# Modulation from float32 blocks, and weight sums made by GpSimd during the input projection

## The chip, the cores and the metric

The kernel runs on one core of a Trainium2 chip. The metric is device time in microseconds (us) of one launch; the median of three runs before the change is 3407.99 us (3407.11 to 3412.31).

## The reference

Two layers of a transformer over 256 context and 1024 latent tokens of width 1024, all in float32. Per layer:

```python
mod = silu(c) @ ada_w + ada_b                     # six rows of 1024: shifts, scales, gates; once for c, once for c_ctx
z = (x * (1 + sc1) + sh1) @ w_in                  # 1024 -> 1984, split into q, kv, k_r, dq, dk, dv and a chunk part
y = concat(mla(q, kv), differential(dq, dk, dv), chunk_mix(zch)) @ w_o
x = layer_norm(ALPHA * x + g1 * y)
u = dwconv3((x * (1 + sc2) + sh2) @ ffn_wup)      # 1024 -> 5632 = gate and value
x = layer_norm(ALPHA * x + g2 * ((silu(gate) * val) @ ffn_wdown))    # 2816 -> 1024
```

## The kernel before, in words

**Arithmetic.** Large products are made from float32 operands that are split in two: `hi`, the value rounded to the fast type float32r (made by ScalarE, in `split`), and `lo`, the rest (`low`, on VectorE or GpSimd). `mm3` issues three matmuls for each product. A few small products are plain float32 matmuls: the chunk mixing in `post_z` (moving operand of 64 elements), the selector in `fin_diff`, `sumj` in `prep_Q`, and the selector `sel4` of the modulation. Every matmul has the line of `mm`, L447; the splits have the lines of `low` (L457) and `copy` (L460).

**Stages**, by the trace in us: start, with eight modulation pieces and the first product of the input projection (0 to 85); input projection of layer 0 (`in_proj`, to 285); attention (to 850); output projection (to 940); up projection (to 1600); down projection (to 1900); the same stages of layer 1 end at about 2080 (input), 2560 (attention), 2680 (output), 3160 (up) and 3410 (down).

**Modulation.** `mod_piece` makes 256 of the 6144 columns of `mod` for both conditioning vectors; there are 24 pieces a layer. A piece loads four blocks of 128x512 of `ada_w` (two of 128x1024 in the eight first ones), splits them, and runs 16 matmuls with the conditioning vector as stationary operand (`s4`: 128 rows x 4 columns) and 256 columns of weights as moving operand, four (or eight) to a task. The result, 4 rows of 256, is copied by ScalarE and brought into columns by two float32 matmuls with `sel4`; VectorE adds the bias (`fin`). Eight pieces stand in the start, 24 are spread over the attention of layer 0 and 16 over that of layer 1, as fillers with a low priority (`MODKEY`).

**Sums of weights.** The up and down projections use a fast matrix multiplication with seven products in place of eight, which needs sums of blocks of weights. Those of the down weights (`db`, four sums of 1408 x 512 a layer) are made by transfers: `sums` and `begin_sums` issue 16 DMAs a layer on GpSimd's queue during the attention, a copy (L591) and then one that adds to it (L592), in chunks of 704 rows. Those of the up weights (S1 to S4 of each of the 22 blocks) are added by VectorE in `up_operand` (`comb`, L1480) just ahead of their splits.

**Order.** `Sched.run` plays the program with a cost for each task, and issues each engine's instructions in the order that comes out; on the chip each engine then works strictly in that order. A task goes to the first of its allowed engines that is free (`either`: VectorE or GpSimd). Buffers come from shared pools: `M` (12 of 128x512), `L` (16 of 128x1024) and `S` among them.

Of the kernel before, what the change touches and what calls it, by code (L numbers as in the profile page):

```python
# [69 lines left out]
SUMROWS = 704  # L70
# [271 lines left out]
def pool_t(n):  # L342
    return {"pool": 2.1e-3 * n + 0.15}
# [47 lines left out]
class Kern:  # L391
# [185 lines left out]
    def flat(self, x, c):  # L577

        return x.rearrange("n p c -> (n p) c")[c * SUMROWS:(c + 1) * SUMROWS]

    def sums(self, l):

        x = self.db[l]
        w = lambda a, b: (lambda: self.i["w_down"][l, a, b])
        out = []

        def make(n, c, a, b, r=()):
            key = ("db", l, n, c)
            put = lambda: self.flat(x[n], c)
            kw = dict(w=[key], key=MODKEY, late=40.0)  # L590
            out.append(lambda: self.s.add({"pool": 1.0}, lambda e: self.nc.gpsimd.dma_start(out=put(), in_=self.flat(a(), c), max_dma_last_dim=2048), (), **kw))  # L591
            out.append(lambda: self.s.add({"pool": 1.0}, lambda e: self.nc.gpsimd.dma_start(out=put(), in_=self.flat(b(), c), accum_op=ALU.add, max_dma_last_dim=2048), [*r, key], **kw))  # L592

        for c in range(NP * P // SUMROWS):
            at = lambda n: ("db", l, n, c)
            make(0, c, w(0, 0), w(0, 1))
            make(1, c, w(0, 1), w(1, 1))
            make(2, c, w(1, 1), lambda: x[0], [at(0)])
            make(3, c, w(1, 0), lambda: x[2], [at(2)])
        return out  # L600

    def begin_sums(self, n):

        for f in self.due[:n]:
            f()
        del self.due[:n]

    def sum_chunks(self, name, l, n, f):
        a, b = f * P * 512, (f + 1) * P * 512 - 1
        m = SUMROWS * 512  # L610
        return [(name, l, n, c) for c in range(a // m, b // m + 1)]
# [28 lines left out]
    def setup(self):  # L640
# [9 lines left out]
        self.s4 = c.tile([P, KD, 4], F32R, tag="s4", name="s4")  # L650
        self.task(act_t(16), lambda e: nc.scalar.activation(s, cc, AF.Silu), ["cT"], ["silu"])
        self.task(dve_t(16), lambda e: nc.vector.tensor_copy(self.s4[:, :, 0:2], s), ["silu"], ["s4a"])
        self.task(dve_t(16), lambda e: self.low(nc.vector, self.s4[:, :, 2:4], s, self.s4[:, :, 0:2]), ["silu", "s4a"], ["s4"])
        self.sel4 = load("sel4", [4, 2])
# [21 lines left out]
        self.dc = d.tile([7, P, NP, P], F32, tag="dc", name="dc")  # L676
        self.db = [d.tile([4, NP, P, HALF], F32, tag=f"db{l}", name="db") for l in range(DEPTH)]
# [5 lines left out]
    def mod_piece(self, l, n, key=0, raws=None):  # L683
        nc = self.nc
        self.s.what = f"mod{l}"
        j, q = QUADS[n // 4], n % 4
        if raws:
            w = [self.weight(None, 1024, self.L, k=4, raw=raws[h]) for h in range(2)]
        else:
            src = [self.mod_src(l, n, h)[:, a:a + 512] for h in range(2) for a in (0, 512)]  # L690
            w = [self.weight(x, 512, self.M, k=2, key=key, acq=True) for x in src]
        kk = KD // len(w)
        ps, m4, pm = self.bank(), self.H(), self.bank(F32, (P, 2, 2))
        for h in range(len(w)):
            def go(e, h=h):
                for k in range(kk):
                    hi, lo = w[h][0][k]()
                    a = self.s4[:, kk * h + k]
                    self.mm(ps[:4, :256], a, hi, h + k == 0, False)
                    self.mm(ps[:4, :256], a, lo, False, kk * h + k == KD - 1)  # L700

            self.task(mm_t(2 * kk, 256), go, ["s4"] + w[h][1], [ps], key=key, acq=[m4] if h == 0 else ())
# [1311 lines left out]
```

## Time and profile before

| | |
|---|---|
| runs, us | 3407.11, 3412.31, 3407.99; median 3407.99 |
| profiled execution, us | 3411.25 |
| its span, first to last instruction, us | 3409.5 |
| mean granted TensorE clock | 0.967 of 2.4 GHz |
| busy: PE, DVE, ACT, POOL | 93%, 79%, 49%, 30% |
| DMA moved | 395 MB, of which 46 MB on GpSimd's queue |

PE is TensorE, PEld its weight loads, DVE VectorE, ACT ScalarE, POOL GpSimd, SP the engine that issues the other DMAs. PEclk is the granted share of TensorE's clock: 1.00 is 2.4 GHz, 0.50 is 1.2 GHz. Busy times of PE run to the modelled end of a matmul and overlap the next one, so the rate of a stretch is read from starts and counts.

### The profile page before, as it was taken

How to read it: one execution, taken by the hardware profiler on the slowest of the kernel's cores; microseconds unless marked ns; L12 is line 12 of the kernel's file. 1: busy time of each engine (PE TensorE's matmuls, PEld its weight loads, DVE VectorE, ACT ScalarE, POOL GpSimd, SP SyncE). 2: the span in 40 equal slices, each digit the busy share in tenths (PEclk: the TensorE clock that was granted, in tenths of full speed). 3: DMA queues.
4: the chain of work that ended last, by engine and by line, in shares of the span. 5: the costliest groups of instructions: out<-in, count | busy, mean ns of one | idle time of the engine just before them, and what ended most of it. 6: DMA issues, size and time to landing. Idle time of an engine off the chain costs nothing. (4 is left out here: it accounts for less than half of the span.)

```text
span 3409.5 us, 53373 instructions
## 1 busy us (share of the span) xinstructions
PE 3186.5 (93%) x18953; PEld 2785.7 (82%) x18953; DVE 2700.5 (79%) x6407; ACT 1677.3 (49%) x2944; POOL 1028.0 (30%) x631
## 2 busy tenths in 40 slices
PE   7999898998988999999999999989999889999997
PEld 5998887887987888887877898878889867877775
DVE  7567887999768787886687757988998788888687
ACT  5125665666244444544444325665662455545542
POOL 3002554543112111121133302554532232322143
PEclk9999998999999999999999999999999999999998
DMA  6214443442312223225663314353423122323672
GB/s 242 72 52 112 118 124 99 126 108 86 121 69 70 89 72 101 87 86 180 210 204 130 116 58 123 92 135 87 119 88 127 62 80 96 107 98 105 229 258 99
DMA packets 258548, 395.40 MB, mean 116 GB/s; under 512 B 63976, under 2 KB 115688, under 8 KB 258280
## 3 DMA queue, kind: packets, MB, share of 16 engines
q1 hardware_dynamic: 240872, 345.84, 31.4%
q0 software_dynamic: 17408, 46.14, 5.9%
q8 instruction: 149, 2.44, 0.3%
q14 instruction: 119, 0.97, 0.1%
HBM read 311.61 MB, written 126.42 MB: 128 GB/s over the span
## 5 line engine op out<-in xcount | busy, mean ns | idle before, releaser
L447 PE MATMUL t<-region 128*128 128x512 f32 (+4 forms) x15631 | 2853.0, 341 | 137.8 <-DVE region L457 55.0
L447 PEld LDWEIGHTS t<-region 128*128 128x128 f32 x15631 | 2442.1, 192 | 480.0 <-DVE region L457 69.2
L457 DVE TENSOR_TENSOR region<-region 128x512 fp32r<-128x512 f32 (+6 forms) x873 | 760.0, 893 | 176.2 <-ACT region L460 122.7
L460 ACT ACTIVATE region<-region 128x512 fp32r<-128x512 f32 (+4 forms) x944 | 593.9, 663 | 382.8 <-PE t L447 132.5
L460 ACT ACTIVATE region<-t 128x512 fp32r<-128x512 f32 (+4 forms) x948 | 462.1, 514 | 600.0 <-PE t L447 386.3
L457 POOL TENSOR_TENSOR region<-region 128x512 fp32r<-128x512 f32 (+7 forms) x283 | 392.3, 1398 | 1109.3 <-ACT region L460 714.8
L1480 POOL TENSOR_TENSOR region<-region 128x512 f32<-128x512 f32 (+3 forms) x132 | 248.6, 1889 | 823.6 <-DVE region L1667 518.5
L1188 ACT ACTIVATE region<-region,q 128x1280 f32<-128x1280 f32 (+1 forms) x216 | 273.5, 1267 | 175.7 <-DVE q L1187 169.7
L1183 DVE TENSOR_SCALAR_CACHE_REDUCE region<-t 128x512 f32<-128x512 f32 (+1 forms) x600 | 333.7, 584 | 21.3 <-PE t L447 19.1
L457 DVE TENSOR_TENSOR region<-t,region 128x512 fp32r<-128x512 f32 (+1 forms) x529 | 296.9, 595 | 52.8 <-ACT region L460 50.9
L1667 DVE SCALAR_TENSOR_TENSOR region<-region,conv 128x1023 f32<-128x1023 f32 x176 | 231.6, 1325 | 36.7 <-ACT region L1665 36.5
L1480 DVE TENSOR_TENSOR region<-region 128x512 f32<-128x512 f32 (+3 forms) x301 | 226.3, 770 | 2.5 <-DMA da<-region 1.4
L1252 PE MATMUL t<-ident,region 128*128 128x128 f32 x1312 | 184.8, 285 | 24.2 <-DVE region L1225 8.1
L1228 POOL TENSOR_TENSOR region<-region 128x1280 f32<-128x1280 f32 (+1 forms) x68 | 186.8, 2746 | 5.7
L1665 ACT ACTIVATE region<-region,conv 128x1024 f32<-128x1024 f32 x88 | 109.2, 1241 | 159.5 <-DVE region L1648 148.3
L1252 PEld LDWEIGHTS t<-ident,region 128*128 128x128 f32 x1312 | 154.9, 147 | 31.8 <-DVE region L1183 11.0
L1227 POOL TENSOR_SCALAR region<-region,q 128x1280 f32<-128x1280 f32 (+1 forms) x68 | 84.5, 1242 | 210.6 <-DVE q L1222 137.7
L447 PE MATMUL t<-region,s 128*4 128x256 f32 x768 | 119.1, 291 | 17.0 <-DVE region L457 9.2
L447 PEld LDWEIGHTS t<-region,s 128*4 128x4 f32 x768 | 64.6, 87 | 47.4 <-DVE region L457 12.5
L548 POOL TENSOR_TENSOR region<-region 128x1024 f32<-128x1024 f32 x26 | 73.7, 2847 | 95.9 <-DMA region<-n 67.7
L1008 DVE TENSOR_TENSOR region<-t,region 128x256 f32<-128x256 f32 x32 | 13.6, 424 | 107.4 <-PE t L447 107.4
L548 DVE TENSOR_TENSOR region<-region 128x1024 f32<-128x1024 f32 x34 | 62.3, 1841 | 18.2 <-DMA region<-n 17.7
(134 smaller groups left out, 1803.5 us busy)
## 6 DMA issues: line engine op xcount, KB each, us to landing
region<-in_wup SPq DMA_DIRECT2D x176, 256.0 KB, 3.0
region<-in_ada_w SPq DMA_DIRECT2D x160, 256.0 KB, 3.1
da<-region SPq DMA_DIRECT2D x154, 256.0 KB, 3.0
region<-da SPq DMA_DIRECT2D x154, 256.0 KB, 4.1
db<-in_w_down POOLq DMA_DIRECT2D x24, 1408.0 KB, 7.5
region<-db SPq DMA_DIRECT2D x88, 256.0 KB, 4.1
region<-in_w_down SPq DMA_DIRECT2D x66, 256.0 KB, 3.9
n<-region SPq DMA_DIRECT2D x26, 512.0 KB, 3.0
```

The source lines that it names most:

```text
L447: self.nc.tensor.matmul(ps, a, b, start=start, stop=stop, skip_group_check=again)
L457: eng.tensor_tensor(out=out, in0=full, in1=hi.bitcast(F32), op=ALU.subtract)
L460: self.nc.scalar.activation(out, in_, AF.Copy, **kw)
L548: self.task(engs or pool_t(D), lambda e, row=row, op=op: self.vec[e].tensor_tensor(out=x[:, :D], in0=x[:, :D], in1=row.t, op=op), [x, row] ...
L1183: self.task(dve_t(b - a), lambda e: nc.vector.tensor_scalar(p[:, a:b], ps[:, :b - a], -scale, None, op0=ALU.mult, op1=ALU.min, accum_out=n ...
L1188: self.task(act_t(nk, 0.19), lambda e: nc.scalar.activation(p[:, :nk], p[:, :nk], AF.Exp, bias=m.t, scale=-1.0, accum_out=s.t), [p, m], [p ...
L1227: nc.gpsimd.tensor_scalar(p2[:, :nk], p2[:, :nk], cc.t, 0.0, op0=ALU.mult, op1=ALU.add)
L1228: nc.gpsimd.tensor_tensor(out=p1[:, :nk], in0=p1[:, :nk], in1=p2[:, :nk], op=ALU.add)
L1252: nc.tensor.transpose(ps[:, u, j * P:(j + 1) * P], B[key][j][:, (kt + u) * P:(kt + u + 1) * P], self.ident)
L1480: self.task(engs or either(n), lambda e: self.vec[e].tensor_tensor(out=o(), in0=a(), in1=b(), op=op), r, w, **kw)
L1665: self.task(act_t(n, 0.15), lambda e: nc.scalar.activation(t.t, u(0, n), AF.Identity, scale=c[:, 1:2], bias=c[:, 3:4]), r + ["conv"], [t])
L1667: self.task(dve_t(n - 1, extra=0.06), lambda e, d=d: nc.vector.scalar_tensor_tensor(t[:, 1 - d:n - d], u(d, n - 1 + d), c[:, 2 * d:2 * d + ...
```

## The change

It has three parts.

1. **Modulation.** The blocks of `ada_w` are used as they are, as stationary float32 operands of 128x128, and the conditioning vectors (`silu`, 2 columns) move. A piece is one task of 16 float32 matmuls with a moving operand of 2 columns. The splits, `s4`, the copy and the selector matmuls are gone.
2. **Sums of down weights.** The 16 adding and copying DMAs a layer are gone. For each of the 11 blocks of down weights, four loads, four adds on GpSimd and four stores are issued among the tiles of the input projection.
3. **Sums of up weights.** For six of the 22 blocks a layer, S1 to S4 are made in the same way and stored in `ws`; the up projection loads them, and VectorE adds only for the other 16 blocks.

```diff
+UP_MADE = 6
...
-    def begin_sums(self, n):
...
+    def sums(self, name, l, m):
+        up = name == "ws"
+        out = (self.ws if up else self.db)[l]
+        src = self.i["wup" if up else "w_down"]
+        z = [self.L(F32, (P, 2, HALF)) for _ in range(2)]
+        for j in range(2):
+            for h in range(2):
+                self.dma(lambda j=j, h=h: z[j][:, h], lambda j=j, h=h: src[l, j, h, m], 4 * P * HALF, w=[(z[j], h)], key=MODKEY)
...
+        order = [("21", "22"), ("t0", "11"), ("21", "11"), ("t1", "12")] if up else [("11", "12"), ("12", "22"), ("t0", "22"), ("t2", "21")]
+        for n, (a, b) in enumerate(order):
+            self.task(pool_t(HALF), lambda e, n=n, a=a, b=b: self.vec[e].tensor_tensor(out=t[n].t, in0=q[a][0](), in1=q[b][0](), op=ALU.add), [q[a][1], q[b][1]], [t[n]], key=MODKEY)
+            self.dma(lambda n=n: out[n, m], lambda n=n: t[n].t, 4 * P * HALF, [t[n]], [(name, l, n, m)], key=MODKEY)
...
     def mod_piece(self, l, n, key=0, raws=None):
...
-                    self.mm(ps[:4, :256], a, hi, h + k == 0, False)
-                    self.mm(ps[:4, :256], a, lo, False, kk * h + k == KD - 1)
...
-                self.mm(pm[:, k], m4[:4, k * P:(k + 1) * P], self.sel4)
...
+        if not raws:
+            raws = [self.load(self.mod_src(l, n, h)[:, a:a + 512], 512, self.M, key) for h in range(2) for a in (0, 512)]
+        kk = KD // len(raws)
+        pm = self.bank(F32, (P, 2, 2))
+        def go(e):
+            for c in range(2):
+                for k in range(KD):
+                    o = k % kk * 256 + c * P
+                    self.mm(pm[:, c], raws[k // kk][:, o:o + P], self.silu[:, k], k == 0, k == KD - 1)
+        self.task({"pe": 1.8}, go, ["silu", *raws], [pm], key=key)
...
     def in_chunk(self, l, name, tabs):
...
+        for n, t in enumerate(tiles):
+            if name != "z" and n % 4 == 1 and self.pairs_due:
+                self.sums("db", l, self.pairs_due.pop(0))
+            if name != "z" and n % 4 == 3 and self.blocks_due:
+                self.sums("ws", l, self.blocks_due.pop(0))
...
     def up_load(self, l, m):
...
+            if f < UP_MADE:
+                todo = [n]
...
+                if x[0] == "S":
+                    j = int(x[1]) - 1
+                    src, r = self.ws[l][j, f], [("ws", l, j, f)]
...
     def up_operand(self, l, m):
...
-        if n[0] == "S":
+        if n[0] == "S" and f >= UP_MADE:
```

**The order on TensorE, where the attention of layer 0 begins** (`s_70` is `s4`, `sel_71` is `sel4`; the last number of a row counts matmuls of the program). Before:

```order
L447 MATMUL t<-region,s_70 4x256 x16
L447 MATMUL t<-sel_71,region 128x2 x2
L447 MATMUL t<-region 128x512 x12
L447 MATMUL t<-region 128x256 x24
L447 MATMUL t<-region,sumj 128x256
L447 MATMUL t<-region 128x256 x27
L447 MATMUL t<-region,s_70 4x256 x12
```

And with the change:

```order
L447 MATMUL t<-silu,region 128x2 x48
L959 MATMUL t<-ident,region 128x128 x6
L447 MATMUL t<-region 128x512 x12
L447 MATMUL t<-region 128x256 x24
L447 MATMUL t<-region,sumj 128x256
L447 MATMUL t<-region 128x256 x27
```

Three whole pieces now stand in a row here; of the 37 others in the attention, two stand together and 35 stand alone, each 16 matmuls without a break, where a piece was in parts of four to sixteen.

**The order on TensorE at the very start**, with the change:

```order
L447 MATMUL t<-silu,region 128x2 x64
L447 MATMUL t<-region 128x512 x36
L447 MATMUL t<-silu,region 128x2 x48
L447 MATMUL t<-region 128x512 x36
L447 MATMUL t<-silu,region 128x2 x16
L447 MATMUL t<-region 128x512 x96
```

The eight pieces stand where they stood before, as runs of 4, 3 and 1 pieces between the first products of the input projection.

**The order on GpSimd in the input projection of layer 0.** Before, with the first DMA at its end and others further on:

```order
L457 TENSOR_TENSOR region<-region 128x768
L929 TENSOR_TENSOR region<-region 128x256 x2
L938 TENSOR_TENSOR region<-region 128x256
L457 TENSOR_TENSOR region<-region 128x1280
L1017 TENSOR_TENSOR region<-region 128x256
L457 TENSOR_TENSOR region<-region 128x1152
L591 DMA db<-in_w_down 704x512
```

And with the change (L591 is now the add of `sums`, L903 the gain in `post_z`):

```order
L591 TENSOR_TENSOR region<-region 128x512 x2
L903 TENSOR_TENSOR region<-region 128x256
L591 TENSOR_TENSOR region<-region 128x512
L903 TENSOR_TENSOR region<-region 128x256
L591 TENSOR_TENSOR region<-region 128x512 x2
L903 TENSOR_TENSOR region<-region 128x256 x2
L591 TENSOR_TENSOR region<-region 128x512 x16
L457 TENSOR_TENSOR region<-region 128x768
L591 TENSOR_TENSOR region<-region 128x512 x44
L457 TENSOR_TENSOR region<-region 128x1152
L591 TENSOR_TENSOR region<-region 128x512 x3
```

All 68 adds of a layer stand ahead of GpSimd's first work for the attention, four gains of `post_z` stand among them, and no DMA is left on this queue.

## Rows read from the trace of the kernel before

**Rows 1.** The page: its first line.
```profile
span 3409.5 us, 53373 instructions
```

**Rows 2.** Busy time by stage: start:end, length, busy us and count by engine, PEclk, DMA.
```profile
core 0: us, PE busy (x) PEld busy (x) DVE busy (x) ACT busy (x) POOL busy (x), PEclk, DMA share, GB/s
0.00:85.00 85.00, 64.79 (x328) 48.07 (x328) 65.08 (x118) 50.27 (x67) 27.36 (x18) 0.94 0.69 243
...
114.00:285.00 171.00, 171.00 (x1286) 170.65 (x1286) 90.89 (x450) 41.24 (x114) 12.41 (x12) 1.00 0.26 76
285.00:850.00 565.00, 513.04 (x3582) 456.39 (x3580) 484.47 (x1455) 354.07 (x699) 261.58 (x173) 0.95 0.40 109
850.00:1100.00 250.00, 226.42 (x1583) 210.39 (x1584) 185.72 (x501) 104.08 (x168) 48.01 (x38) 0.95 0.25 83
...
1900.00:2080.00 180.00, 175.21 (x1265) 171.32 (x1264) 106.93 (x482) 43.64 (x110) 22.47 (x18) 0.98 0.29 87
2080.00:2560.00 480.00, 445.54 (x3121) 396.21 (x3119) 434.14 (x1233) 301.08 (x561) 221.51 (x137) 0.97 0.40 107
```

**Rows 3.** Groups on PE, shapes apart: two of 285:850, then two of 2080:2560.
```profile
L447 PE MATMUL t<-region,s 128*4 128x256 f32 x381 | 60.3, 291 | 5.2 <-DVE region L457 4.0 <-ACT region L460 1.1
L447 PE MATMUL t<-sel,region 4*128 4x2 f32 x96 | 15.0, 257 | 1.2 <-ACT region L460 0.6 <-DVE region L457 0.5
...
L447 PE MATMUL t<-region,s 128*4 128x256 f32 x244 | 38.0, 286 | 3.6 <-DVE region L457 3.6
L447 PE MATMUL t<-sel,region 4*128 4x2 f32 x64 | 9.6, 251 | 2.3 <-ACT region L460 2.3
```

**Rows 4.** Timeline of PE in the start: start, us, what, count, [idle before].
```profile
6.55 0.37 PE L447 MATMUL t<-region,s 128*4 128x256 f32 x1 [6.55 <-ACT region L460]
...
21.15 0.60 PE L447 MATMUL t<-sel,region 4*128 4x2 f32 x4 [0.52 <-ACT region L460]
...
38.96 2.20 PE L447 MATMUL t<-region,s 128*4 128x256 f32 x16
41.09 0.60 PE L447 MATMUL t<-sel,region 4*128 4x2 f32 x4
...
85.23 35.03 PE L447 MATMUL t<-region 128*128 128x64 f32 x190 [7.48 <-issue]
```

**Rows 5.** Busy time by stretch, as rows 2, for five short stretches.
```profile
35.60:41.60 6.00, 5.97 (x49) 4.15 (x47) 3.31 (x5) 4.80 (x7) 3.81 (x2) 1.00 0.81 286
85.20:88.60 3.40, 3.37 (x16) 3.40 (x16) 3.40 (x21) 0.00 (x0) 0.00 (x0) 0.50 0.00 0
95.10:98.20 3.10, 3.10 (x15) 2.57 (x14) 3.02 (x14) 0.00 (x0) 0.72 (x1) 0.99 0.35 140
419.40:429.60 10.20, 6.19 (x33) 6.19 (x34) 1.32 (x2) 1.38 (x3) 3.74 (x3) 0.50 0.59 200
467.20:470.60 3.40, 3.40 (x16) 3.10 (x15) 3.40 (x17) 3.18 (x7) 0.45 (x1) 0.50 0.57 155
```

**Rows 6.** Timeline of POOL, 400:435, as rows 4.
```profile
421.11 0.70 POOL L591 DMA_DIRECT2D db<-in_w_down  x1 [10.19 <-issue]
421.82 3.04 POOL L457 TENSOR_TENSOR region<-region 128x640 fp32r<-128x640 f32 x2
```

**Rows 7.** PE's waits in 285:850, then in 2080:2560: total us, times, longest.
```profile
PE t L1117 <- POOL region L457: 14.0, 2, 7.5
...
PE t L447 <- POOL region L457: 5.0, 1, 5.0
```

**Rows 8.** Groups of 285:850, shapes apart: two on DVE, one on POOL, one on ACT.
```profile
L457 DVE TENSOR_TENSOR region<-t,region 128x512 fp32r<-128x512 f32 x174 | 112.1, 680 | 25.0 <-ACT region L460 24.6
...
L457 DVE TENSOR_TENSOR region<-region 128x512 fp32r<-128x512 f32 x32 | 28.6, 901 | 0.4 <-ACT region L460 0.3
...
L457 POOL TENSOR_TENSOR region<-region 128x512 fp32r<-128x512 f32 x62 | 82.7, 1345 | 142.1 <-ACT region L460 127.5 <-PE t L1252 7.4 <-DVE q L1220 5.2
...
L460 ACT ACTIVATE region<-region 128x512 fp32r<-128x512 f32 x95 | 57.2, 628 | 0.2
```

**Rows 9.** The page, groups of the whole run: VectorE's and GpSimd's adds.
```profile
L1480 POOL TENSOR_TENSOR region<-region 128x512 f32<-128x512 f32 (+3 forms) x132 | 248.6, 1889 | 823.6 <-DVE region L1667 518.5
...
L1480 DVE TENSOR_TENSOR region<-region 128x512 f32<-128x512 f32 (+3 forms) x301 | 226.3, 770 | 2.5 <-DMA da<-region 1.4
```

More of the change, by code (lines that the diff above doesn't have):

```diff
@@ L574, in row_from_col @@
         return row
[L577 to L600, printed above, removed]
@@ L676, in setup @@
         self.dc = d.tile([7, P, NP, P], F32, tag="dc", name="dc")
+        self.ws = [d.tile([4, UP_MADE, P, HALF], F32, tag=f"ws{l}", name="ws") for l in range(DEPTH)]
         self.db = [d.tile([4, NP, P, HALF], F32, tag=f"db{l}", name="db") for l in range(DEPTH)]
@@ L686, in mod_piece @@
         j, q = QUADS[n // 4], n % 4
[L687 to L698, printed above, removed]
-                    self.mm(ps[:4, :256], a, hi, h + k == 0, False)
-                    self.mm(ps[:4, :256], a, lo, False, kk * h + k == KD - 1)
-            self.task(mm_t(2 * kk, 256), go, ["s4"] + w[h][1], [ps], key=key, acq=[m4] if h == 0 else ())
-        self.task(act_t(256), lambda e: self.copy(m4[:4], ps[:4, :256]), [ps], [m4], key=key)
-        def sel(e):
-            for k in range(2):
-                self.mm(pm[:, k], m4[:4, k * P:(k + 1) * P], self.sel4)
-        self.task({"pe": 0.25}, sel, [m4, "sel4"], [pm], key=key)
+        if not raws:
[8 more added lines that the diff above has]
+        self.task({"pe": 1.8}, go, ["silu", *raws], [pm], key=key)
         ks = slice(2 * q, 2 * q + 2)
@@ L843, in in_proj @@
         tabs = self.tabs if l == 0 else self.z_tables(l)
+        self.pairs_due, self.blocks_due = list(range(NP)), list(range(UP_MADE))
         for name in ZCH:
@@ L891, in in_chunk @@
             tiles = (8, 9, 0, 1) if l == 0 else (6, 7, 8, 9, 2, 3, 4, 5)
-        for t in tiles:
+        for n, t in enumerate(tiles):
[3 more added lines that the diff above has]
+                self.sums("ws", l, self.blocks_due.pop(0))
             r = self.in_tile(l, name, t, wk, wb, tabs)
@@ L1902, in program @@
             ada = [lambda a=a: self.mod_piece(*a, MODKEY) for a in ada]
-            self.due = self.sums(l)
-            m, d = len(ada), len(self.due)
-            fill = []
-            for j, a in enumerate(ada):
-                fill += [lambda: self.begin_sums(1)] * ((j + 1) * d // m - j * d // m) + [a]
-            self.attention(l, fill)
+            self.attention(l, ada)
             self.out_tiles(l, NT, True)
@@ L1997, in _arrays @@
     a["sel64"] = np.tile(np.eye(64, dtype=np.float32), (2, 1))
-    a["sel4"] = np.tile(np.eye(2, dtype=np.float32), (2, 1))
     return {k: np.ascontiguousarray(v) for k, v in a.items()}
```

36 lines of the change are left out of this document (16 added, 20 removed).

## The prediction, made before the changed kernel had run

> **What bounds the kernel now.** The page gives a span of 3409.5 us [rows 1]; the profiled execution itself took 3411.25 us, 3.3 above the median of the runs, 3407.99. The sum below is made against 3411.25 and 3 is taken off at its end.
>
> I read the busy time by stage next, since the mean over the span hides which engine sets which stage [rows 2]. The reader is to see that TensorE sets the input projection almost alone: 171.0 us busy of 171 in layer 0, 175.2 of 180 in layer 1, with VectorE near half. In the attention TensorE is busy 513.0 of 565 us and 445.5 of 480, with a clock of 0.95 and 0.97, and VectorE 484.5 and 434.1: two engines close to full, so what TensorE gains or loses there counts nearly in full and what VectorE gains counts in part. The first 250 us of the up projection have TensorE at 226.4 and VectorE at 185.7. Then come the groups of the modulation, TensorE's start, short stretches around falls of its clock, and the waits on GpSimd, each where it is needed.
>
> **The new piece of modulation.** Forty pieces stand in the attention, where TensorE is near the bound, 24 in layer 0 and 16 in layer 1. An old piece took 2.13 us of wide matmuls and 0.60 for its selector in an undisturbed place at full clock, 2.7 together [rows 4]. By busy time it is (60.3 + 15.0) / 24 = 3.1 and (38.0 + 9.6) / 16 = 3.0 [rows 3]. I take 2.8. The new one has 16 float32 matmuls. A float32 matmul leaves two records: two selector matmuls a piece make 48 over 24 pieces, and the row counts 96 [rows 3]. So a piece is 32 records, each with 128 columns of weights to load. The nearest such rows are the plain float32 matmuls of 64 elements, 16 records in 3.40 us at half clock, 0.21 each [rows 5], hence an estimated 0.11 at full clock; four selector records with 2 elements take 0.60, 0.15 each [rows 4], so a short moving operand is no cheaper and the load of the weights sets the pace. A piece is 32 x 0.11 + 0.1 = 3.6 us, 0.8 more than before: 40 x 0.8 = **+32** (+20 with an old piece of 3.1, +36 with 2.7). Against this stands the Trainium skill, "TensorE: Matmul & The Clock Gate", section "Back-to-back issue gap": its table of gaps between matmuls gives one of up to 64 columns an issue floor of about 25 ns. By it the piece would be 32 x 0.025 = 0.8 us and the term about -80; the rows with short operands here do not show it.
>
> **The clock around a piece.** TensorE runs at 2.4 GHz or at 1.2. A run of 32 short matmuls has no counterpart in this trace in the middle of full work; the four-row, 256-wide pieces at 35.6 us ran with a clock of 1.00 [rows 5]. The nearest thing to 2-wide matmuls is the 64-wide float32 run at 85.2 us: the engine is busy 3.37 of 3.40 us and yet the granted clock is 0.50 [rows 5], and it is 0.99 at 95.1 [rows 5]. The new pieces are most like that run, so I take it that most of them cost a fall. Falls in this trace last from 3.4 us (467.2) to 10.2 us (419.4) [rows 5], and half of the work in them is lost: 1.7 to 3.4 us where it is TensorE that is busy 3.4 to 6.2 us. The lower end for a piece is nothing. I take 2.0, nearest to the short fall, since work around a piece is dense: 40 x 2.0 = **+80** (0 to 136).
>
> **The start.** TensorE ran the first four old pieces from 6.55 us to 21.75 [rows 4], about 15.2 us. As 4 x 32 records at half clock, 0.21 each, they take 27.2: +12. The next four take 22 in place of 10 to 11: +12 (at full clock only +4). Two falls after them, +3. Against this the splits and the copies that ran between the pieces are gone and a gap of 7.5 us at 85.2 [rows 4] may be filled: -9. **+18** (-5 to +30).
>
> **GpSimd behind its DMA issues.** The add of `begin_sums` was issued after 10.2 us of idle time with a split of two tiles behind it [rows 6]. GpSimd goes strictly in order, so the split waits for a transfer that has nothing to do with it, and TensorE waits for the split: 14.0 us in two waits of layer 0, 5.0 in one of layer 1 [rows 7]. The fall of the clock in such a place had TensorE busy 6.19 us at half clock [rows 5], 3.1 lost; for all three I take 8. No DMA is left on that queue: **-27** (-19 for the waits alone, -30 at most).
>
> **Relief in the attention.** The split of the pieces goes: 28.6 us on VectorE in layer 0, 82.7 us on GpSimd, and ScalarE's 57.2 us of roundings [rows 8]; layer 1 has two thirds of the pieces. A VectorE split from SBUF operands takes 901 ns where one with an operand in PSUM takes 680 [rows 8], so VectorE also loses time next to a busy GpSimd, and gets some back. What can be won is bounded by what TensorE stands idle, 52 + 34.5 = 86.5 us, less the 19 counted above: 67; and by the half clock of these stages, 0.05 x 565 + 0.03 x 480 = 43, less 8: 35 [rows 2]. From 0 to -102; with nothing to say which waits are really for VectorE's total load, I take half, **-50**.
>
> **The up projection.** Six blocks a layer lose four VectorE adds each, at 0.77 us [rows 9]. It counts where TensorE is not full, in the first two or three blocks of a layer: 20 x 0.77 = 15. The others are hidden by TensorE. **-8** (0 to -17).
>
> **The input projection.** GpSimd gets 17 x 4 = 68 adds a layer, 1.35 us (its split, [rows 8]) to 1.89 (its add, [rows 9]) each: 92 to 128 us in stages of 171 and 180, where it was busy 12.4 and 22.5 [rows 2]. They fit. What covers them is TensorE's own full load; if the cover is gone, GpSimd's splits of the attention stand behind the last adds and are late by the rest. The transfers are 68 loads and 68 stores of 256 KB, 35.6 MB, 208 GB/s on top of 76; the start ran 243 at a share of 0.69 [rows 2], so there is room, with some weight blocks later than now. VectorE pays for GpSimd: at 0.22 us more (901 - 680) for each of its 450 and 482 instructions it would come to 190 us in 171 and 213 in 180: +52 as the upper end. Only some of its instructions meet an add, so I take **+8** (0 to +52). The 46 MB taken off GpSimd's queue in the attention is put at nothing: the DMA share there is 0.40 [rows 2], and the transfers were hidden but for the waits counted.
>
> **Sum.** 32 + 80 + 18 - 27 - 50 - 8 + 8 = +53: 3464, and 3461 on the scale of the median. About 0.2%, 7 us, is what a measurement of this kernel can tell from no change.
>
> **Rivals.**
> *The clock holds* through a piece of 3.6 us, as it held through the 256-wide pieces. For it: the pieces in the attention mostly stand alone between dense matmuls. Against: the 64-wide run had half clock while busy. Then the second term is 0 and the start costs less, -5: 3411 + 32 - 5 - 27 - 50 - 8 + 8 = 3361, and 3358 after the 3 are off. Chance 0.16. It decides between slower and faster: with my other terms the change gains below 27 us for 40 pieces, about 0.7 us a piece.
> *Short matmuls are cheap*, 0.8 us a piece, the weights loaded as fast as they are issued. The first term is then 40 x (0.8 - 2.8) = -80 in place of +32 and a clock fall cannot come from so short a run, the start -15: about 3286. The selector's 0.15 us a record speaks against it. Chance 0.04.
> *GpSimd's adds hold up VectorE* in the input projection, so that the upper end, +52, comes in place of +8: 3505. For it: 901 against 680 ns, and strict order on GpSimd, where four gains of `post_z` stand among the adds and wait for their loads. Against: VectorE is half idle there. Chance 0.12.
> The forecast itself has 0.68, with its own range of 3415 to 3505 (0.6 to 3 us for the clock and half of the relief either way).
>
> **How the numbers follow.** Slower by over 0.2% is all of the case of the adds (0.12) and 0.60 of the forecast's 0.68, whose lower tail reaches the present time: 0.72. Faster is the two cheap cases (0.20) and 0.03 of that tail: 0.23. The rest, 0.05, lies within 0.2%. The range of 8 in 10 goes from 3350, which takes in the case of a held clock to just below its middle, to 3510, which takes in the case of the adds; it leaves out the cheap matmuls and the outer parts of the rest.
>
> **What would show it.** In the profile after, the groups should hold 1536 records of float32 matmuls with a moving operand of 2, some 0.11 us apart (0.21 at half clock); a spacing of 0.03 would be the cheap case. The granted clock of the attention should fall from 0.95 and 0.97 to about 0.90, with falls that begin in the pieces; if it stays, the held clock was right. TensorE should reach the 64-wide float32 run later than at 85 us. The wait of line 1117 on GpSimd's split should be gone, and the input projection still last 171 to 180 us with TensorE full; if VectorE's adds and splits there grow by 0.2 us and TensorE shows gaps, it is the case of the adds. The forecast is wrong as a whole if the clock does not fall at the pieces, or if the attention turns out to follow VectorE's load rather than TensorE's.

## The result and the profile after

The change took 3518.01 us (median of 4 runs, 3511.0 to 3521.76) against 3409.84 for the kernel before in the same series: a ratio of 1.0315, 95% interval 1.0295 to 1.0335. The forecast was 3461 with a range up to 3510. The direction was right and the time lies above the range.

The first lines of the page and busy time by stage, of the changed kernel (columns as in [rows 2]). The stretches are, in this order: the start; input projection, attention and begin of the up projection of layer 0; input projection, attention with output projection and begin of the up projection of layer 1.

```profile
span 3514.1 us, 54631 instructions
...
0.00:102.50 102.50, 91.59 (x424) 82.46 (x425) 38.98 (x103) 28.20 (x40) 12.55 (x14) 0.92 0.65 220
102.50:316.60 214.10, 196.17 (x1353) 190.46 (x1353) 142.83 (x539) 41.72 (x103) 95.50 (x76) 0.94 0.63 211
316.60:927.80 611.20, 585.02 (x3991) 549.81 (x3990) 460.77 (x1465) 309.50 (x604) 181.94 (x110) 0.90 0.23 69
987.30:1143.20 155.90, 138.39 (x943) 126.31 (x942) 112.57 (x263) 76.56 (x130) 35.54 (x27) 0.96 0.25 83
1921.30:2164.70 243.40, 218.69 (x1434) 206.92 (x1433) 174.66 (x631) 67.37 (x146) 115.84 (x93) 0.94 0.63 212
2164.70:2724.60 559.90, 531.15 (x3659) 494.60 (x3658) 443.94 (x1361) 282.45 (x518) 175.05 (x96) 0.92 0.22 67
2724.60:2902.40 177.80, 156.39 (x1003) 140.79 (x1002) 142.98 (x302) 82.31 (x129) 57.32 (x31) 0.95 0.31 104
```

Against [rows 2] two things stand out. The input projection of layer 0, where TensorE was busy 171.0 of 171 us, now has it at 196.17 of 214.10. And the attention's clock is 0.90 and 0.92, where it was 0.95 and 0.97.

To see where each microsecond went, the stages must begin and end with the same work. Both traces have 17993 matmul records beside those of the modulation; without the 144 of the selector in `fin_diff` they are 17849. I number these, cut both traces where the records of the same number start (a few neighbours have changed places at a cut), and split each difference into idle time of TensorE, half clock (one minus the granted clock, times the length) and the rest, which is work:

| stage | before | after | difference | idle | half clock | rest |
|---|---|---|---|---|---|---|
| start, to the 64-wide float32 run | 85.2 | 102.5 | +17.3 | -9.5 | +3.2 | +23.6 |
| input projection 0 | 189.2 | 214.1 | +24.9 | +17.9 | +7.0 | 0.0 |
| attention 0 | 581.7 | 611.2 | +29.5 | -25.9 | +32.4 | +23.0 |
| begin of up 0 | 166.9 | 155.9 | -11.0 | -5.9 | -4.0 | -1.1 |
| rest of layer 0 | 838.8 | 837.7 | -1.1 | +0.8 | -4.5 | +2.6 |
| input projection 1 | 215.8 | 243.3 | +27.5 | +17.9 | +11.9 | -2.3 |
| attention and output 1 | 528.7 | 560.0 | +31.3 | -10.2 | +29.0 | +12.5 |
| begin of up 1 | 187.2 | 177.7 | -9.5 | -4.1 | -3.4 | -2.0 |
| rest of layer 1 | 601.6 | 597.6 | -4.0 | -3.2 | -3.4 | +2.6 |

So: start +17, input projections +52, attention +61, and 26 back in the up and down projections; 105 in all, the difference of the two spans (3514.1 and 3409.5).

**Inside an input projection.** Groups on VectorE of the kernel before, 85 to 275 us, the stretch of the input projection of layer 0:

```profile
L497 DVE SCALAR_TENSOR_TENSOR q<-q 128x1 f32<-128x1 f32 x73 | 16.8, 234 | 1.5
L499 DVE TENSOR_TENSOR q<-q 128x1 f32<-128x1 f32 x73 | 11.3, 156 | 1.6
L498 DVE TENSOR_SCALAR q<-q 128x1 f32<-128x1 f32 x73 | 10.9, 151 | 1.6
```

The same groups of the changed kernel, 102 to 317 us:

```profile
L497 DVE SCALAR_TENSOR_TENSOR q<-q 128x1 f32<-128x1 f32 x73 | 26.8, 371 | 1.6
L499 DVE TENSOR_TENSOR q<-q 128x1 f32<-128x1 f32 x74 | 21.0, 288 | 1.7
L498 DVE TENSOR_SCALAR q<-q 128x1 f32<-128x1 f32 x74 | 10.8, 150 | 1.7
```

These are the norm's reciprocal root (`rsqrt1`), one element per partition. L498 has one tensor operand and is unchanged; L497 and L499, with two or three, became longer. The timelines of the changed kernel show how, first VectorE, then GpSimd and TensorE (columns as in [rows 4]):

```profile
247.24 1.33 DVE L497 SCALAR_TENSOR_TENSOR q<-q 128x1 f32<-128x1 f32 x1
248.60 0.15 DVE L498 TENSOR_SCALAR q<-q 128x1 f32<-128x1 f32 x1
248.79 1.03 DVE L499 TENSOR_TENSOR q<-q 128x1 f32<-128x1 f32 x1
249.86 1.21 DVE L497 SCALAR_TENSOR_TENSOR q<-q 128x1 f32<-128x1 f32 x1
251.10 0.15 DVE L498 TENSOR_SCALAR q<-q 128x1 f32<-128x1 f32 x1
251.29 1.00 DVE L499 TENSOR_TENSOR q<-q 128x1 f32<-128x1 f32 x1
252.32 1.30 DVE L497 SCALAR_TENSOR_TENSOR q<-q 128x1 f32<-128x1 f32 x1
...
256.61 0.22 DVE L497 SCALAR_TENSOR_TENSOR q<-q 128x1 f32<-128x1 f32 x1
```

```profile
247.26 7.56 POOL L591 TENSOR_TENSOR region<-region 128x512 f32<-128x512 f32 x6 [3.86 <-ACT region L919]
```

```profile
256.57 0.37 PE L969 MATMUL t<-identr,region 128*128 128x128 f32 x1 [5.57 <-DVE q L495]
```

Six adds of 1.26 us run back to back, and during them each multiplication of one element takes 1.0 to 1.3 us instead of 0.16 to 0.22: each ends within 0.06 us of the end of an add (at 248.52, 249.78 and so on, counted from 247.26). A chain that needs 1.9 us when nothing disturbs it (the next one, from 256.61) took 7.6. TensorE waits for a tile that VectorE makes right behind this chain, in the order in which its work was issued, and stood still 5.57 us. The longest wait of the two input projections, 7.97 us in layer 1 at 1969.59, stands behind the same thing: eight adds back to back, and, right ahead of the matmul, two instructions of `post_z` on VectorE (L903, 128x256, two SBUF operands) at 1.37 us each, where undisturbed ones take 0.41. The Trainium skill, "SBUF — State Buffer", section "Who interferes with whom", says that a VectorE instruction with two SBUF inputs contends with a GpSimd instruction that reads SBUF, and calls such contention an exclusive lock; this trace agrees, with 1.33 us for one element beside a 1.26 us add.

**Around a modulation piece** in the attention of layer 0, busy time of the stretches ahead of a piece, of the piece and of its fall:

```profile
616.00:619.00 3.00, 3.00 (x31) 3.00 (x30) 2.82 (x6) 2.08 (x6) 0.82 (x1) 1.00 0.05 11
619.06:622.55 3.49, 3.49 (x34) 3.49 (x33) 0.78 (x2) 0.58 (x3) 0.69 (x1) 1.00 0.05 8
623.43:626.84 3.41, 3.41 (x18) 3.41 (x17) 0.42 (x1) 0.00 (x0) 0.00 (x0) 0.50 0.69 233
```

The piece itself is 3.49 us, 32 records 0.112 us apart, at full clock. The fall comes 0.9 us after its end and lies on the dense matmuls behind it. The 40 pieces of the attentions make 37 runs (one of three, one of two), and only two of these have no half clock in the 9 us from their start. Of the other 35, 18 have the fall begin after the last record has started (by up to 1.6 us), 15 within the run, as early as 2.2 us after its start, and two start while the clock is already low. Counted in the records of the clock, the attention of layer 0 has 23 falls with 126 us at half clock where it had 10 with 61, and that of layer 1 18 with 92 where it had 7 with 34. What TensorE did before them differs: ahead of each of the 17 falls of the kernel before there are 1.1 to 3.3 us of idle time in the last 6 us; of the 41 with the change 34 have records of pieces there instead, and 31 of these no idle time (0.05 us at most).

The long waits on GpSimd [rows 7] are gone; of what TensorE waits for in the attention of layer 0 of the changed kernel, 316.6 to 927.8 us, these lines stand first (columns as in [rows 7]):

```profile
PE t L447 <- DVE region L457: 15.8, 10, 4.2
PE t L447 <- DVE region L1157: 4.5, 6, 2.2
PE t L1226 <- ACT region L1162: 1.9, 1, 1.9
```

### The profile page after: what moved, and what is told of

Same layout as the page of the kernel before. It is cut to its first block, busy times and chain, and to the rows that moved or that the text cites. A ratio compares the mean times of both kernels' runs of the same rounds, so it can differ in the third digit from the quotient of the medians.

```text
span 3514.1 us, 54631 instructions
## 1 busy us (share of the span) xinstructions
PE 3313.5 (94%) x19529; PEld 2955.8 (84%) x19529; DVE 2639.1 (75%) x6279; ACT 1567.0 (45%) x2726; POOL 1039.4 (30%) x632
## 5 line engine op out<-in xcount | busy, mean ns | idle before, releaser
L447 PE MATMUL t<-region 128*128 128x256 f32 (+4 forms) x15631 | 2876.5, 344 | 137.2 <-DVE region L457 59.7
L447 PEld LDWEIGHTS t<-region 128*128 128x128 f32 x15631 | 2474.8, 195 | 478.6 <-DVE region L457 69.0
L457 DVE TENSOR_TENSOR region<-region 128x512 fp32r<-128x512 f32 (+6 forms) x796 | 697.9, 901 | 191.5 <-ACT region L460 150.0
L460 ACT ACTIVATE region<-t 128x512 fp32r<-128x512 f32 (+3 forms) x906 | 449.7, 523 | 748.1 <-PE t L447 408.1
L460 ACT ACTIVATE region<-region 128x512 fp32r<-128x512 f32 (+4 forms) x768 | 481.6, 661 | 334.8 <-PE t L447 150.9
L457 POOL TENSOR_TENSOR region<-region 128x512 fp32r<-128x512 f32 (+7 forms) x184 | 253.6, 1388 | 873.6 <-ACT region L460 294.8
L447 PEld LDWEIGHTS t<-silu,region 128*128 128x128 f32 x1536 | 213.7, 226 | 6.3 <-issue 5.3
L447 PE MATMUL t<-silu,region 128*128 128x2 f32 x1536 | 213.1, 274 | 5.4 <-DMA region<-in_ada_w 5.3
L591 POOL TENSOR_TENSOR region<-region 128x512 f32<-128x512 f32 x136 | 179.3, 1335 | 104.5 <-DMA region<-in_w_down 41.7
L1454 DVE TENSOR_TENSOR region<-region 128x512 f32<-128x512 f32 (+3 forms) x255 | 178.9, 719 | 3.1 <-POOL region L1454 2.4
L1226 PEld LDWEIGHTS t<-ident,region 128*128 128x128 f32 x1312 | 166.9, 155 | 15.8 <-ACT region L1162 5.6
```

What stands on the lines that cost most here:

```text
L447: self.nc.tensor.matmul(ps, a, b, start=start, stop=stop, skip_group_check=again)
L457: eng.tensor_tensor(out=out, in0=full, in1=hi.bitcast(F32), op=ALU.subtract)
L460: self.nc.scalar.activation(out, in_, AF.Copy, **kw)
L591: self.task(pool_t(HALF), lambda e, n=n, a=a, b=b: self.vec[e].tensor_tensor(out=t[n].t, in0=q[a][0](), in1=q[b][0](), op=ALU.add), [q[a][ ...
L1226: nc.tensor.transpose(ps[:, u, j * P:(j + 1) * P], B[key][j][:, (kt + u) * P:(kt + u + 1) * P], self.ident)
L1454: self.task(engs or either(n), lambda e: self.vec[e].tensor_tensor(out=o(), in0=a(), in1=b(), op=op), r, w, **kw)
```

## The experiments

The same ledger holds for each run against the kernel before. Its four sums, in us (the last column is everything from the output projection of layer 0 to the down projection, and from the up projection of layer 1 on). It is a ledger of the one profiled execution of each run, and the four executions of e3, e4, e6 and e7 lie 18 to 24 us apart, so a few us in a column say nothing:

| run | time, us | ratio to before (95%) | start | input projections | attentions | up and down |
|---|---|---|---|---|---|---|
| the change | 3518.0 | 1.0315 (1.0295 to 1.0335) | +17 | +52 | +61 | -26 |
| e1, old pieces | 3427.1 | 1.0054 (1.0038 to 1.0071) | -9 | +46 | -5 | -17 |
| e2, new pieces alone | 3532.2 | 1.0358 (1.0342 to 1.0374) | +19 | -2 | +74 | +27 |
| e3, no adds | 3469.2 | 1.0182 (1.0152 to 1.0212) | +15 | +7 | +55 | -18 |
| e4, pieces in parts | 3476.9 | 1.0194 (1.0171 to 1.0217) | +13 | +51 | +29 | -26 |
| e5, old pieces, VectorE's adds | 3390.5 | 0.995 (0.9933 to 0.9967) | -6 | +17 | -7 | -25 |
| e6, half adds | 3503.4 | 1.0266 (1.0239 to 1.0292) | +20 | +26 | +67 | -19 |
| e7, one up block | 3504.4 | 1.0277 (1.0247 to 1.0307) | +18 | +23 | +66 | -6 |
| e8, down sums in the up projection | 3468.1 | 1.0168 (1.0152 to 1.0183) | -6 | +12 | -6 | +57 |
| e9, the same on VectorE | 3395.3 | 0.9961 (0.9946 to 0.9976) | -7 | +12 | -16 | -7 |
| e10, no sums | 3401.5 | 0.998 (0.9971 to 0.999) | +1 | +4 | -10 | +1 |

**Old pieces (e1).** The functions of the modulation are those of before; everything else is the change's.

```diff
-        pm = self.bank(F32, (P, 2, 2))
...
+            w = [self.weight(x, 512, self.M, k=2, key=key, acq=True) for x in src]
...
+                    self.mm(ps[:4, :256], a, hi, h + k == 0, False)
+                    self.mm(ps[:4, :256], a, lo, False, kk * h + k == KD - 1)
```

> The change with the modulation pieces as they were before (splits, four-row stationary operand, selector); the sums of weights as in the change. Theory A (the loss has two separate sources: the new pieces cost 17 us in the start and some 85 in the attention before what is won back there, and GpSimd's adds cost 52 in the two input projections by holding up VectorE): start 0, input projections +52, attention about -25 (no split behind a DMA issue any more), up projection about -20, so 3410 + 52 - 25 - 20 = about 3417, 3405 to 3430. Rival B (the new pieces cost little, the attention is late because it starts behind a late input projection and its VectorE work is behind): the time stays above 3480.

Measured 3427: the input projections keep +46, the attentions come back to -5 and the start to -9. The two losses are separate, and rival B (above 3480) falls. (Why the start is shorter than before was not followed.)

**New pieces alone (e2).** `mod_piece` and its constants from the change, in the kernel before.

```diff
-                    self.mm(ps[:4, :256], a, hi, h + k == 0, False)
...
+                    self.mm(pm[:, c], raws[k // kk][:, o:o + P], self.silu[:, k], k == 0, k == KD - 1)
```

> The kernel before with the new modulation pieces alone; sums of weights by transfers and by VectorE as before. Theory A: start +17, input projections 0, attention +61 as measured in the change plus the 15 to 25 us of waits behind DMA issues that are not removed here, up projection 0: 3410 + 17 + 80 = about 3507, 3490 to 3520, with the granted clock of the attention at 0.90 and 0.91 as in the change. Rival B: below 3450.

Measured 3532, 12 above the stated bound; rival B (below 3450) falls. Start and input projections are as expected, and the attentions nearly so (+74). The 27 us in the up and down projections, which have no modulation, no theory had, and this was not followed further. In the attentions the half clock grows by 67, the idle time shrinks by 28 and the work grows by 35 us.

One part of the expectation failed. The waits behind DMA issues were to stay, since the transfers stay on GpSimd's queue, and GpSimd still stands idle ahead of one. But TensorE's wait of [rows 7] on GpSimd's split is gone (L1104 is the L1117 of before). A line of GpSimd's timeline, then of TensorE's waits, 293.1 to 916.5 us, both of this run:

```profile
570.71 0.71 POOL L591 DMA_DIRECT2D db<-in_w_down  x1 [9.46 <-issue]
...
PE t L1104 <- DVE region L457: 0.2, 1, 0.2
```

So the DMA issue alone did not cost those 14.0 us: with the old pieces' splits off GpSimd it cost TensorE no such wait.

**No adds (e3).** All transfers stay.

```diff
...
-            self.task(pool_t(HALF), lambda e, n=n, a=a, b=b: self.vec[e].tensor_tensor(out=t[n].t, in0=q[a][0](), in1=q[b][0](), op=ALU.add), [q[a][1], q[b][1]], [t[n]], key=MODKEY)
-            self.dma(lambda n=n: out[n, m], lambda n=n: t[n].t, 4 * P * HALF, [t[n]], [(name, l, n, m)], key=MODKEY)
+            self.dma(lambda n=n: out[n, m], lambda n=n: z[n // 2][:, n % 2], 4 * P * HALF, [(z[n // 2], n % 2)], [(name, l, n, m)], key=MODKEY)
```

> The change without the 68 adds a layer on GpSimd: the four stores of each block store the loaded blocks themselves, so the sums of the down weights and of six up blocks are left out and all transfers stay. Theory A (an add on GpSimd holds VectorE's instructions with two SBUF operands until it ends, and the one-element chain of the norms at 247 us waited so six times): the input projections lose the 52 us almost wholly, 3518 - 45 = about 3473, 3460 to 3485; the mean of the one-element L497 in the first input projection goes from 371 ns back to about 234. Rival C (the 136 transfers a layer and the order of SP's queue make the input projection late): 3505 or more.

Measured 3469; the input projections fall from +52 to +7 with the same transfers, and the chain's group is nearly back (VectorE, 102 to 300 us):

```profile
L497 DVE SCALAR_TENSOR_TENSOR q<-q 128x1 f32<-128x1 f32 x78 | 19.4, 251 | 2.1
```

Rival C falls: what the loads and stores cost in the input projections is within those 7 us.

**Pieces in parts (e4).**

```diff
...
+        for c in range(2):
+            for h in range(2):
+                ks = range(4 * h, 4 * h + 4)
+                self.task({"pe": 0.9}, lambda e, c=c, ks=ks: go(e, c, ks), ["silu", *raws], [pm], key=key)
```

> The change with each modulation piece as four tasks of four matmuls (eight records, 0.9 us) in place of one task of sixteen, so that most stand apart among other matmuls. Theory A (a piece of 3.5 us in one run lets the clock fall to half for 3.4 us or more, nearly each time): most falls of the attention go, the clock there returns from 0.90 and 0.91 to about 0.95 and 0.96, the records stay at 0.112 us; 50 of the 61 us of half clock that the attention gained are worth some 40: about 3475, 3460 to 3490. Rival D (the loss is in the loads of the weights, 0.112 us a record, and the clock falls for other reasons, such as VectorE being late): 3510 or more, the clock as in the change.

Measured 3477, as expected, and rival D (3510 or more) falls; the attentions go from +61 to +29. But the clock comes back in part only: 22 falls in place of 41, 174 us at half clock in place of 219 (before: 17 and 96). Busy time by stretch of this run, the two attentions:

```profile
317.00:920.00 603.00, 575.43 (x3994) 543.47 (x3993) 464.77 (x1457) 310.68 (x606) 181.33 (x116) 0.91 0.23 70
2149.00:2685.00 536.00, 515.11 (x3658) 480.60 (x3657) 439.85 (x1362) 281.58 (x515) 178.06 (x98) 0.94 0.23 69
```

Layer 0 stays at 0.91, where 0.95 was expected. The unbroken run of a piece is a cause of falls, and not all of it: 16 of the 22 falls have two to four parts of a piece in the 6 us ahead of them, and the other six have none, but 1.8 to 3.2 us of idle time. The 16 parts of 0.9 us that stand alone, with no other within 6 us, are followed by no fall in 6 us (one of them lies in a fall that had begun before).

**Adds on VectorE (e5).** The run with the old pieces, and one word.

```diff
-            self.task(pool_t(HALF), lambda e, n=n, a=a, b=b: self.vec[e].tensor_tensor(out=t[n].t, in0=q[a][0](), in1=q[b][0](), op=ALU.add), [q[a][1], q[b][1]], [t[n]], key=MODKEY)
+            self.task(dve_t(HALF), lambda e, n=n, a=a, b=b: self.vec[e].tensor_tensor(out=t[n].t, in0=q[a][0](), in1=q[b][0](), op=ALU.add), [q[a][1], q[b][1]], [t[n]], key=MODKEY)
```

> As the run with the old modulation pieces (3427), but the 68 adds a layer are on VectorE in place of GpSimd. Theory A (GpSimd's adds cost the input projections 46 us by holding VectorE): nearly all of it returns, though VectorE now does some 49 us of adds in each input projection, 108 + 49 of 189 us, and TensorE may wait a little: 3427 - 46 + 5 to 15 = about 3391, 3378 to 3405, faster than the kernel before. Rival C (transfers and SP's order): 3420 or more.

Measured 3390.5, 0.5% faster than the kernel before and the lowest time here (e9, 3395.3, is not clearly apart from it). VectorE carries the adds of the input projection itself, and TensorE loses 17 us there in place of 46. Group on VectorE, 79 to 277 us, busy time of the same stretch, and busy time of the same stage of e1:

```profile
L591 DVE TENSOR_TENSOR region<-region 128x512 f32<-128x512 f32 x67 | 49.8, 755 | 6.3 <-DMA region<-in_w_down 4.7 <-DMA region<-in_wup 1.1
```

```profile
79.40:277.00 197.60, 192.65 (x1353) 187.66 (x1353) 149.84 (x577) 43.15 (x106) 39.15 (x34) 0.97 0.68 226
...
76.20:283.40 207.20, 192.00 (x1354) 186.81 (x1353) 144.22 (x538) 45.59 (x110) 104.71 (x77) 0.97 0.67 221
```

VectorE is busier than in e1, from which the run differs by that word alone (149.84 of 197.60 against 144.22 of 207.20 us), and the stage is shorter. It was not VectorE's load that made it late.

**Half adds (e6).**

```diff
...
+            for c in (slice(0, 256), slice(256, 512)):
+                self.task(pool_t(256), lambda e, n=n, a=a, b=b, c=c: self.vec[e].tensor_tensor(out=t[n][:, c], in0=q[a][0]()[:, c], in1=q[b][0]()[:, c], op=ALU.add), [q[a][1], q[b][1]], [(t[n], c.start)], key=MODKEY)
```

> The change with each add on GpSimd cut into two of 256 elements, 136 a layer; transfers as in the change. Theory A1 (a VectorE instruction with two SBUF operands waits until the GpSimd add that is under way ends, and then goes): the one-element L497 and L499 that are held take about 0.65 us in place of 1.0 to 1.3, and the input projections lose about half as much: 3518 - 25 = about 3493, 3480 to 3505. Rival E (VectorE and GpSimd share the memory's rate, so the loss goes with the elements added and not with the length of one add): unchanged, 3510 to 3522.

Measured 3503, inside theory A1's range but near its upper end, with executions from 3489 to 3509; the time alone hardly speaks against rival E, and the stages decide. The input projections lose 26 in place of 52, as theory A1 has it, and the attentions lose 6 more than in the change. Timelines of this run, GpSimd and VectorE:

```profile
240.68 5.60 POOL L592 TENSOR_TENSOR region<-region 128x256 f32<-128x256 f32 x8
```

```profile
243.56 0.66 DVE L497 SCALAR_TENSOR_TENSOR q<-q 128x1 f32<-128x1 f32 x1
244.25 0.15 DVE L498 TENSOR_SCALAR q<-q 128x1 f32<-128x1 f32 x1
244.44 0.47 DVE L499 TENSOR_TENSOR q<-q 128x1 f32<-128x1 f32 x1
244.94 0.66 DVE L497 SCALAR_TENSOR_TENSOR q<-q 128x1 f32<-128x1 f32 x1
```

Eight adds of 0.70 us hold one element for 0.47 to 0.66 us: the hold shrinks with the single add, as it must if an instruction waits for the end of the add under way. By rival E, a shared rate, the stage would have lost as much as before, since as many elements are added.

**One up block (e7).**

```diff
-UP_MADE = 6
+UP_MADE = 1
```

> The change with S1 to S4 made ahead for one up block a layer in place of six: 48 adds on GpSimd a layer in place of 68. Theory A (the adds cost the input projections 52 us in all, by their number; the six blocks gain 20 to 24 us in the up projections): input projections 52 x 20 / 68 = 15 less, up projections 17 to 20 more: 3518 + 3 = about 3521, 3508 to 3535. Rival F (the up blocks' gain is not from these adds but from the order that comes with them): up projections unchanged, about 3503.

Measured 3504, where 3521 was expected. That is rival F's number, but not by its way: the gain in the up projections goes from 26 to 6, as theory A said. But 20 adds fewer take away 30 of the 52 us in the input projections, not 15: the cost does not follow the number of adds, though the holds nearly do (in the first input projection the instructions of the chain that took over 0.4 us went from 24 to 16, with 48 adds a layer in place of 68). By the ledger the adds for five up blocks a layer cost more on GpSimd, 30 us, than the 20 that they bring; the whole times (3496 to 3515 against 3511 to 3522) bear this out only weakly.

**Down sums in the up projection (e8), and the same on VectorE (e9).** From the run with the old pieces; adds of the up blocks on VectorE in both.

```diff
-            if name != "z" and n % 4 == 1 and self.pairs_due:
-                self.sums("db", l, self.pairs_due.pop(0))
...
                 self.blocks[f - 1] = self.blocks[f] = None
+                self.sums("db", l, f // 2)
...
-            self.task(pool_t(HALF), lambda e, n=n, a=a, b=b: self.vec[e].tensor_tensor(out=t[n].t, in0=q[a][0](), in1=q[b][0](), op=ALU.add), [q[a][1], q[b][1]], [t[n]], key=MODKEY)
+            self.task((dve_t if up else pool_t)(HALF), lambda e, n=n, a=a, b=b: self.vec[e].tensor_tensor(out=t[n].t, in0=q[a][0](), in1=q[b][0](), op=ALU.add), [q[a][1], q[b][1]], [t[n]], key=MODKEY)
```

> As the run with the old modulation pieces (3427), but the 24 adds of the up blocks are on VectorE in the input projection and the 44 adds of the down weights on GpSimd in the up projection, whose TensorE is full for 567 us with VectorE busy 430. Theory A (what a held VectorE costs depends on whether TensorE waits for VectorE in that stage): input projections +5 to 10, start -9, attention -5, up projections -20 and +5 to 10 for the holds: about 3390, 3375 to 3405. Rival G (44 holds of 1.3 us cost as much in the up projection as in the input projection, 34 us): about 3415 or more.

> As the run with the down weights' adds in the up projection (3468), but these 44 adds a layer on VectorE in place of GpSimd; the same loads, stores and buffers in the same place. Theory A (GpSimd's adds hold VectorE there too: the convolutions of 1023 elements went from 1335 to 1503 ns and the splits from 882 to 996 ns in layer 1): VectorE has 430 + 32 of 567 us, and most of the 66 us that the up and down projections lost against the kernel before return: about 3400, 3385 to 3420. Rival H (the loads, stores and twelve more buffers of the sums displace the up projection's own loads and buffers): 3450 or more.

Measured 3468 for e8: rival G, and more than it said; why it is more than its 34 us was not followed. The up and down projections lost 57 us, 44 of them in the rest of layer 1, where TensorE had been busy 571.9 of 601.5 us in the kernel before. With the same transfers and buffers and the adds on VectorE (e9, 3395) they gained 7. Groups on VectorE, layer 1's up projection, first of e8 (2700 to 3200 us), then of e9 (2690 to 3190 us):

```profile
L457 DVE TENSOR_TENSOR region<-region 128x512 fp32r<-128x512 f32 x167 | 163.5, 996 | 21.0 <-ACT region L460 18.5 <-PE t L447 1.4
L1661 DVE SCALAR_TENSOR_TENSOR region<-region,conv 128x1023 f32<-128x1023 f32 x84 | 124.8, 1503 | 27.9 <-ACT region L1659 27.9
...
L1628 DVE SCALAR_TENSOR_TENSOR t<-t,region 128x512 f32<-128x512 f32 x22 | 15.1, 688 | 0.4 <-PE t L447 0.3
```

```profile
L457 DVE TENSOR_TENSOR region<-region 128x512 fp32r<-128x512 f32 x201 | 177.1, 902 | 31.6 <-ACT region L460 22.0 <-PE t L447 4.7 <-issue 3.6
L1661 DVE SCALAR_TENSOR_TENSOR region<-region,conv 128x1023 f32<-128x1023 f32 x88 | 116.7, 1337 | 24.2 <-ACT region L1659 23.1 <-DMA region<-in_w_down 0.7
...
L1628 DVE SCALAR_TENSOR_TENSOR t<-t,region 128x512 f32<-128x512 f32 x22 | 15.1, 686 | 0.0
```

The convolution and the splits, which read two SBUF operands, take 166 and 94 ns more on average; L1628, which reads one from PSUM, does not. Rival H falls.

**No sums (e10).** The kernel before without its transfers on GpSimd's queue; the sums are left out.

```diff
-            self.due = self.sums(l)
+            self.due = []
...
-            return (lambda: self.db[l][self.DB[i], p]), self.sum_chunks("db", l, self.DB[i], p)
+            return (lambda: self.i["w_down"][l, 0, 0, p]), []
```

> The kernel before without the 16 transfers a layer on GpSimd's queue; the down projection reads blocks of the down weights in place of their sums, so the sums are left out. It measures by itself what a GpSimd held by its DMA issues cost. Step of the prediction (-27): about 3382, 3378 to 3390. Theory A2 (the gain is 10 to 20 us in layer 0, where the two long waits stood, and nothing in layer 1, since the change and the runs with the old pieces show layer 1's attention no faster): about 3396, 3390 to 3402. No gain would be 3405 to 3415.

Measured 3401.5, a ratio of 0.998: a gain of 6 us (3 to 10 by the interval), within the range of theory A2. In the profiled execution, the slowest of the ten (3407.35), the attention of layer 0 is 20 us shorter, as A2 has it, and that of layer 1 is not unchanged but 10 us longer, with 7 more at half clock and 4 more idle. Why layer 1 loses when transfers leave GpSimd's queue stays open; e1, e5 and e8 show the same (+6 to +11), e9 hardly (+2). That it hangs on the order that the scheduler then finds is a guess.

## Why the prediction failed

| term | forecast | measured | from |
|---|---|---|---|
| new pieces, work | +32 | +35 | rest in both attentions, e2 |
| falls around pieces | +80 | +67 | half clock in both attentions, e2 |
| start | +18 | +17 | ledger |
| GpSimd behind DMA issues | -27 | -10 | both attentions, e10 |
| relief in the attention | -50 | -28 | idle time in both attentions, e2 |
| up projections | -8 | -26 | ledger; 20 of them by e7 |
| input projections | +8 | +52 | ledger, e3, e5 |
| sum | +53 | +107 | |

The measured terms of the attention come from runs with one part of the change alone; together, 35 + 67 - 10 - 28 = +64, they stand beside the +61 of the change. The -10 and the -28 are not clean of each other, though: the long waits of [rows 7] are gone both in e10 and in e2, so part of the agreement is luck. What the removed transfers brought beside the new pieces is read from e2 and the change, +74 and +61: 13 us.

**Right:** the price of a piece (3.49 us against 3.6 forecast, records 0.112 us apart and 0.213 at half clock), that nearly every piece costs a fall (though half of the falls begin behind the pieces and not in them), and the start, whose first four pieces took 27.4 us against 27.2. The 25 ns issue floor that the prediction weighed, from the Trainium skill, "TensorE: Matmul & The Clock Gate", section "Back-to-back issue gap", is a lower bound that these records stay far above, at 112 ns; the same section says that its formula for the gap has no time for loading the stationary operand, which each of these records has to load.

**Wrong, and the step that failed:** "Only some of its instructions meet an add, so I take **+8**". The price of a meeting was taken as 0.22 us, the difference of two group means [rows 8]. Such a mean is made of many undisturbed instructions and few held ones: here 24 instructions of the chain in layer 0 took over 0.4 us (2 in the kernel before), 1.06 on average, and the others 0.19 as before. And the cover was argued from "TensorE's own full load" and, against the rival, from VectorE's, half of the stage. What TensorE waits for stands on VectorE behind a chain of dependent one-element instructions, each of which can be held by the next add. So the rival of the adds (3505, chance 0.12) came true in the input projections. That its upper end, +52, is the measured number is luck: it was to come from VectorE being busy longer than the whole stage, and VectorE was busy 142.83 of 214.10 and 174.66 of 243.40 us. The argument against, "VectorE is half idle there", was no argument; e5 has VectorE busier than e1 and the stage 10 us shorter.

**Mis-sized:** the wins of the attention. The step "with nothing to say which waits are really for VectorE's total load, I take half" had a row that could have said more: TensorE's wait on VectorE's splits in layer 0, 17.8 us in the kernel before (275 to 856 us) and 15.8 after the change:

```profile
PE t L447 <- DVE region L457: 17.8, 18, 2.6
```

Taking 28.6 us of splits from VectorE and 82.7 from GpSimd shortened it by 2, and 4.0 of the 17.8 were the old pieces' own [rows 3]. The -27 assumed that a removed wait gives its whole length and its fall back, and layer 1 returned neither. It also put down to the DMA issues alone waits that are gone as well with the pieces' splits off GpSimd (e2): up to 19 of the -28 are those same waits.

**Mis-sized the other way:** the up projections, -8 against -26. The chosen half rested on TensorE covering all but the first blocks. It was in just these first stretches that 20 of the 26 us came, over a third of it from falls of the clock that no longer happened (idle -5.9 and -4.1, half clock -4.0 and -3.4), which the step had not priced.

Errors of +44 (input projections) and +39 (wins of the attention that did not come) on one side and of -18 (up projections) and -13 (falls) on the other make 52 of the 54 us between the two sums.

**Slips in the working.** The time of the cheap matmuls, 3286, leaves out the -50; with it, it is 3236. The upper end of the falls, 136, takes 3.4 us a piece, where half of the 6.2 us of busy TensorE is 3.1. The 1.89 us for GpSimd's add is a mean over four shapes [rows 9]; the adds of 512 elements took 1.26 back to back. The bracket of the forecast's own range (0.6 to 3 us a piece, half of the relief) gives 3380 to 3526 with its ends added, not 3415 to 3505, and would have held the measured time.

## What to carry to other kernels

Before work is moved to GpSimd, look in the stage that it moves to for short VectorE instructions with two SBUF operands that stand in a dependent chain ahead of a matmul: each can take as long as a whole GpSimd instruction (here 1.33 us for 0.22), and neither a low busy share of VectorE nor a full TensorE covered that here. Adding 50 us of adds a layer to VectorE itself was cheaper here by 29 us (e1 against e5) than putting the same adds beside it. And price a changed matmul together with the clock behind it: 35 us of more work in the pieces brought 67 us of half clock with them (e2).

## What was not expected of the hardware

- A VectorE instruction on one element per partition took 1.33 us beside a GpSimd add of 1.26 us, against 0.16 to 0.22 us without; beside GpSimd adds of 0.70 us alone it took at most 0.78 (e6). An instruction with one of its two operands in PSUM kept its time (L1628, 688 and 686 ns in e8 and e9).
- The clock can fall after the piece and not in it: the piece shown ran at full clock for 3.49 us, and the half clock of 3.41 us began 0.9 us after its end, on matmuls that kept TensorE busy without a gap. So it was in 18 of 35 runs of pieces; in 15 the fall began within the run.
- A run of two-column matmuls that keeps TensorE busy without a gap, as in these 3.49 us, was met by half clock within 9 us of its start in 35 of 37 cases; with the pieces cut into parts, 22 falls remained in the attentions, and none followed a part of 0.9 us that stood alone.
